# A decoder block on one core: other weight-ring depth and instruction order in the U stage, another one-hot layout, groups of 4 at the end of V, more gathers in U

## The chip, the cores and the metric

The kernel runs on one core of a Trainium2 chip. The metric is the device time in microseconds (us) of one execution. The core has one matrix engine (TensorE, "PE" in the profile, with its weight loads as "PEld"), a vector engine (VectorE, "DVE"), a scalar engine (ScalarE, "ACT"), GpSimd ("POOL") and SyncE ("SP"), which here only issues DMAs. Each engine works through its own list of instructions in order.

## The reference, cut to what matters

The block is attention and an mLSTM side by side, an output projection, and then PEER, a product-key mixture of 16,384 one-row experts, which takes some two thirds of the time:

```python
q  = (ht @ w_q).reshape(T, HEADS, 2, SUB)              # T = 528 token rows, 512 of which are output
s  = einsum('thpd,hpnd->thpn', q, sub_keys)            # scores of 2 x 128 sub-keys per head
...                                                    # top 16 of each side, then top 16 of the sums
idx, gate                                              # (T, 8 heads x 16), gate = softmax of the best
act = gelu(einsum('td,tkd->tk', hb, u[idx]))           # u, v: 16384 x 2048 f32
y   = einsum('tk,tkd->td', gate * act, v[idx])
out = rmsnorm(x + y)
```

## The kernel before, in words

Two ways of computing PEER stand side by side. 352 of the tokens go the dense way: all 16,384 experts are computed for them on TensorE, and a gate matrix G (expert x token, nearly all zero) picks the right ones. The other 128 + 32 tokens go the sparse way: for each of their picks POOL gathers one expert row per partition (L836, 128 rows of 8 KB, about 1.05 MB) and DVE multiplies it with the token and sums (L844, "dot"), or adds it with a weight to the result (L857, "axpy"). There are 320 such gather steps (NJ), first those of u, then those of v. A planner (`run`, `pace`, JU) spreads them: JU of them are to be done by the end of the U stage, the rest in V. At most 3 rows are in flight (buffers "ug").

The dense way has two stages.

*U* goes through 128 chunks of 128 experts. For each chunk `step` computes u·h for 352 tokens with 48 f32 matmuls (16 k-tiles, each as high·high, low·high and high·low part of the operands, L89 to L91), `u_chunk` applies GELU on ACT (L889) and stores the result to DRAM (Ad, L890). The weights come in two halves of 512 KB a chunk: `load_half` issues the DMA on SP (L72) into one of 3 raw buffers, `split_half` makes the high part on ACT (L79, `hid`) and the low part on DVE (L80, `lod`); 5 buffers each for high and low. Chunks 0 to 31 run beside the routing (top-k; `t2b` and `t3` sum the ids out of one-hots on POOL, L969, and DVE, L974). Chunks 32 to 121 ("U main") carry the building of G: a group of 4 tokens at a time, `ebuild` makes one-hot matrices `e` (is_equal, L1076 and L1077), the weighted `eg` on DVE (L1079) and `ea` on ACT (L1081), and `gbuild` multiplies them on TensorE (12 bf16 matmuls of 128 columns, L1092), copies the product on ACT to a staging tile `stg` (L1093, a single buffer of 2 MB) and every 8 groups stores it to DRAM (Gd, L1095). Chunks 122 to 127 (UTAIL) run beside the first preparations of V.

*V* goes through 256 halves of v. For each group of chunks (GROUPS) the operands act = GELU x G are loaded from Ad and Gd (`p_load`: gt, av), multiplied (`p_mul`: tm) and split (`p_split`: ah, al). All groups but the last run in transposed form (`tmm`: 24 matmuls of 352 columns a half, the weights being the v half); at the end of a group `yadd` adds the PSUM banks to yT on DVE (L1287). The last group runs in row form (`vmm`: token rows out, 18 matmuls of 512 columns a half), and `part` and `finish` turn its sums into the normalized output.

The order of most engines is set by a scheduler inside the program; POOL is in written order from U main on. With the change ACT is, too. The kernel's functions that the diff touches:

Of the kernel before, what the change touches and what calls it, by code (L numbers as in the profile page):

```python
# [8 lines left out]
F = mybir.dt.float32  # L9
# [5 lines left out]
OP = mybir.AluOpType  # L15
# [26 lines left out]
NQ = 128 // NB  # L42
SB = 128 // NQ
ND = S - 128 - NB
GROUPS = [8] + [16] * 7 + [8]
NJ = 2 * (128 + SB)
JU = 150
AR = 20
AR1 = 8

# [1 line left out]
def bcast(ap, n):  # L52
    return bass.AP(tensor=ap.tensor, offset=ap.offset, ap=[list(a) for a in ap.ap] + [[0, n]])
# [7 lines left out]
def body(tc, I, out):  # L61
    nc = tc.nc
    top = ExitStack()
    with top:
# [3 lines left out]
        dp = top.enter_context(tc.tile_pool(name="dp", bufs=1, space=DRAM))  # L68

        def load_half(src, name, rawp=None):  # L70
            raw = (rawp or wp).tile([128, 8, 128], F, name="raw" + name, tag="raw", bufs=3)
            nc.sync.dma_start(raw, src.rearrange("p (k c) -> p k c", k=8))  # L72
            return raw

        def split_half(src, name, raw=None, eng=nc.vector):
            raw = raw or load_half(src, name)
            hi = wp.tile([128, 8, 128], R, name="hi" + name, tag="whi")
            lo = wp.tile([128, 8, 128], R, name="lo" + name, tag="wlo")
            nc.scalar.copy(hi, raw)  # L79
            eng.tensor_tensor(lo, raw, hi.bitcast(F), op=OP.subtract)  # L80
            return hi, lo

        def split_tile(src, name):
            return [split_half(src[b], f"{name}_{b}") for b in range(2)]

        def mm3(ps, w, k, xh, xl, cs):
            hi, lo = w[k // 8]
# [578 lines left out]
def rest(tc, I, out, L):  # L666
# [204 lines left out]
    sp = [I["wq"][i] for i in range(16)] + [I["u"][c] for c in range(NK)]  # L871
    w[2] = split_tile(sp[2], "d2")

    def step(n, mid=None):
        if n + 1 < len(sp):
            w[n + 1] = split_tile(sp[n + 1], f"d{n + 1}")
        ps = pmu.tile([128, 512], F, name="pu", tag="pu")
        nn = S if n < 16 else ND
        for k in range(KD):
            mm3(ps[:, :nn], w[n], k, h2h, h2l, slice(0, nn))  # L880
            if k == 7 and mid:
                mid()
        w.pop(n)
        return ps

    def u_chunk(c, mid=None):
        ps = step(16 + c, mid)
        at = h2p.tile([128, ND], F, name="at", tag="at", bufs=3)
        nc.scalar.activation(at, ps[:, :ND], AF.Gelu)  # L889
        nc.scalar.dma_start(Ad[c // 4, :, c % 4, :], at)  # L890

    with tc.tile_pool(name="tk", bufs=1) as tk, \
            tc.tile_pool(name="pss", bufs=2, space=PSUM) as pss, \
# [33 lines left out]
        def head_tasks(h, b):  # L927
            st = {}
            cs = slice(16 * h, 16 * h + 16)

            def grid(dst, lo, hi):
                o = 0
                for i in range(5):
                    n = 16 // (i + 1)
                    nc.gpsimd.tensor_tensor(dst[:, o:o + n], lo[:, :n], bcast(hi[:, i], n), op=OP.add)
                    o += n
                nc.gpsimd.tensor_tensor(dst[:, o:o + 6].rearrange("p (a c) -> p a c", c=2), bcast_mid(lo[:, :2], 3),
                                        bcast(hi[:, 5:8], 2), op=OP.add)
                nc.gpsimd.tensor_tensor(dst[:, o + 6:o + 14], hi[:, 8:16], bcast(lo[:, 0], 8), op=OP.add)

            bv = (gsel if b == 3 else gs[:, b])[:, cs]

            def t1():
                sv = tk.tile([128, 2, 16], F, name="sv", tag="sv", bufs=3)
                si = tk.tile([128, 2, 16], U32, name="si", tag="si", bufs=3)
                st["sv"], st["si"] = sv, si
                return [(sv[:, p, :], si[:, p, :], hd[h, p][:, b, :]) for p in range(2)]

            def t1b():
                sv, si = st["sv"], st["si"]  # L950
# [12 lines left out]
            def t2b():
                bpb = tk.tile([128, 16], BF, name="bpb", tag="bpb", bufs=3)
                nc.vector.tensor_copy(bpb, st["bp"])
                eq = tk.tile([128, NCAND, 16], BF, name="eqb", tag="eqb", bufs=2)
                nc.vector.tensor_tensor(eq, iom, bcast_mid(bpb, NCAND), op=OP.is_equal)
                oh = tk.tile([128, NCAND, 16], F, name="oh", tag="oh", bufs=2)
                nc.gpsimd.tensor_tensor(oh, eq, bcast(st["cd"][:, 1, :], 16), op=OP.mult)  # L969
                st["oh"] = oh  # L970

            def t3():
                oh = st["oh"]
                nc.vector.tensor_reduce(ids[:, b, cs], oh.rearrange("p c k -> p k c"), axis=AX.X, op=OP.add)  # L974
# [88 lines left out]

    with tc.tile_pool(name="gk", bufs=1, reuse_waits="tile") as gk, \
            tc.tile_pool(name="psg", bufs=2, space=PSUM) as psg, \
            tc.manual_schedule(engines={mybir.EngineType.Pool}):
        stg = {}

        ge = {}

        def ebuild(q):
            t0 = 4 * q
            e = gk.tile([128, 2, 128, 4], BF, name="e", tag="e", bufs=2)
            eg = gk.tile([128, 2, 128, 4], BF, name="eg", tag="eg", bufs=2)
            ea = gk.tile([128, 4, 128], BF, name="ea", tag="ea", bufs=2)
            nc.vector.tensor_tensor(e[:, 0], iota4, bcast_mid(n1T[:, t0:t0 + 4], 128), op=OP.is_equal)  # L1076
            nc.vector.tensor_tensor(e[:, 1], iota4, bcast_mid(n2T[:, t0:t0 + 4], 128), op=OP.is_equal)  # L1077
            for i in range(2):
                nc.vector.tensor_tensor(eg[:, i], e[:, 1], bcast_mid(gp[:, 1 + i, t0:t0 + 4], 128), op=OP.mult)  # L1079
            for j in range(4):  # L1080
                nc.scalar.activation(ea[:, j, :], e[:, 1, :, j], AF.Copy, scale=g0[:, t0 + j:t0 + j + 1])  # L1081
            ge[q] = e[:, 0], [ea.rearrange("p j n -> p n j"), eg[:, 0], eg[:, 1]]

        def gbuild(q):
            tg, r = divmod(4 * q, TG)
            if r == 0:
                stg[tg] = gk.tile([128, NK, TG], F, name="stg", tag="stg")
            e1, eg = ge.pop(q)
            pg = psg.tile([128, 4, 128], F, name="pg", tag="pg")
            for j in range(4):  # L1090
                for i in range(3):
                    nc.tensor.matmul(pg[:, j, :], e1[:, :, j], eg[i][:, :, j], start=(i == 0), stop=(i == 2))  # L1092
            nc.scalar.copy(stg[tg][:, :, r:r + 4], pg.rearrange("p j n -> p n j"))  # L1093
            if r + 4 == TG:
                nc.sync.dma_start(Gd[tg, :, 0:NK, :], stg[tg])  # L1095
# [6 lines left out]
        ebuild(0)  # L1102

        def pace(c):
            run(n0 + int((c + 1 - c0) * (JU - n0) / (NK - c0)))

        for c in range(ci, NK - UTAIL):
            u_chunk(c)
            while ng < min(ND // 4, (c + 1 - ci) * (ND // 4) / (NK - 12 - ci)):
                gbuild(ng)  # L1110
                ng += 1
                if ng < ND // 4:
                    ebuild(ng)
            pace(c)
    sU.close()

    with ExitStack() as sV:
        vp = sV.enter_context(tc.tile_pool(name="vp", bufs=1, side="right", reuse_waits="tile"))
        pool_order = sV.enter_context(tc.manual_schedule(engines={mybir.EngineType.Pool}))
        g0s = [sum(GROUPS[:g]) for g in range(len(GROUPS) + 1)]  # L1120
        gts, ats, tms, A = {}, {}, {}, {}

# [70 lines left out]
        for c in range(NK - UTAIL, NK):  # L1193
# [270 lines left out]
```

## Time and profile before

| what | us |
|---|---|
| median of 3 runs (lowest, highest) | 3330.11 (3321.87, 3330.35) |
| profiled execution, time | 3331.74 |
| profiled execution, span of the trace | 3330.0 |
| PE busy, share of span | 3264.0, 98% |
| DVE busy | 2320.2, 70% |
| ACT busy | 1325.5, 40% |
| POOL busy | 943.9, 28% |
| DMA traffic | 815.47 MB, mean 245 GB/s |

In stages, by the trace: projections, attention, mLSTM and the query projection until about 1000 us; routing beside U chunks until 1412; U main until 2210; UTAIL until 2264; V in transposed form until 3239.9; the row form of the last group until 3317; then the last normalization and store. Mean granted TensorE clock is 0.992 of full. PE's busy time is a union of pipelined matmuls, so the distance from start to start, not the duration of one, tells what an instruction costs the engine.

### The profile page before, as it was taken

How to read it: one execution, taken by the hardware profiler on the slowest of the kernel's cores; microseconds unless marked ns; L12 is line 12 of the kernel's file. 1: busy time of each engine (PE TensorE's matmuls, PEld its weight loads, DVE VectorE, ACT ScalarE, POOL GpSimd, SP SyncE). 2: the span in 40 equal slices, each digit the busy share in tenths (PEclk: the TensorE clock that was granted, in tenths of full speed). 3: DMA queues.
4: the chain of work that ended last, by engine and by line, in shares of the span. 5: the costliest groups of instructions: out<-in, count | busy, mean ns of one | idle time of the engine just before them, and what ended most of it. 6: DMA issues, size and time to landing. Idle time of an engine off the chain costs nothing.

```text
span 3330.0 us, 51020 instructions
## 1 busy us (share of the span) xinstructions
PE 3264.0 (98%) x20126; PEld 3067.1 (92%) x20126; DVE 2320.2 (70%) x3504; ACT 1325.5 (40%) x2219; POOL 943.9 (28%) x942
## 2 busy tenths in 40 slices
PE   8999999999999999999999999997999999999998
PEld 7889898888887899999999999997999999999996
DVE  7444444444367788787877778767888888888973
ACT  5444444453252233444544544433333333333323
POOL 2011111110015566423332233322323323323312
PEclk8999999999999999999999999998999999999999
DMA  4222121123353266588888978999999999999972
GB/s 154 70 70 77 64 77 64 64 70 115 127 186 136 87 221 226 206 323 316 332 343 325 361 297 348 354 362 337 377 354 375 372 365 370 375 364 372 379 279 101
DMA packets 230162, 815.47 MB, mean 245 GB/s; under 512 B 21697, under 2 KB 85697, under 8 KB 186529
## 3 DMA queue, kind: packets, MB, share of 16 engines
q1 hardware_dynamic: 105488, 400.72, 33.3%
q0 software_dynamic: 46080, 335.56, 25.7%
q10 hardware_dynamic: 78352, 75.92, 6.8%
q8 instruction: 158, 2.59, 0.3%
q14 instruction: 84, 0.68, 0.1%
HBM read 757.33 MB, written 54.79 MB: 244 GB/s over the span
## 4 chain that ended last, share of the span: by engine, by line
PE 85%; DVE 8%; DMA 2%; issue 2%; ACT 1%; POOL 1%; ACTq 0%; SPq 0%; POOLq 0%; DVEq 0%
PE pu L89 10%; PE pu L90 10%; PE pu L91 10%; PE py L1275 8%; PE py L1277 8%; PE py L1276 8%; PE ps L89 5%; PE ps L91 5%; PE ps L90 5%; PE pg L1092 3%; PE po L742 2%; PE po L740 2%; PE po L741 2%; DVE y L857 1%; DVE lov L80 1%
## 5 line engine op out<-in xcount | busy, mean ns | idle before, releaser
L89 PE MATMUL pu<-hh,hid 128*128 128x352 f32 (+1 forms) x2272 | 759.8, 334 | 0.2 <-ACT at L889 0.2
L90 PE MATMUL pu<-hh,lod 128*128 128x352 f32 (+1 forms) x2272 | 751.3, 331 | 3.1 <-DVE lod L80 3.1
L91 PE MATMUL pu<-hl,hid 128*128 128x352 f32 (+1 forms) x2272 | 750.2, 330 | 0.0
L1275 PE MATMUL py<-ah,hiv 128*128 128x352 f32 x1920 | 627.0, 327 | 20.5 <-ACT hiv L79 9.5
L1276 PE MATMUL py<-ah,lov 128*128 128x352 f32 x1920 | 623.4, 325 | 8.8 <-DVE lov L80 8.8
L1277 PE MATMUL py<-al,hiv 128*128 128x352 f32 x1920 | 625.5, 326 | 0.0
L79 ACT CAST hiv<-rawv 128x1024 fp32r<-128x1024 f32 x256 | 269.2, 1053 | 572.4 <-PE py L1277 462.6
L80 DVE TENSOR_TENSOR lod<-rawd,hid 128x1024 fp32r<-128x1024 f32 x284 | 361.0, 1287 | 176.7 <-ACT hid L79 175.5
L90 PEld LDWEIGHTS pu<-hh,lod 128*128 128x128 f32 x2272 | 428.2, 188 | 12.8 <-DVE lod L80 3.4
L89 PEld LDWEIGHTS pu<-hh,hid 128*128 128x128 f32 x2272 | 429.9, 189 | 10.3 <-ACT at L889 0.8
L91 PEld LDWEIGHTS pu<-hl,hid 128*128 128x128 f32 x2272 | 428.1, 188 | 9.7
L79 ACT CAST hid<-rawd 128x1024 fp32r<-128x1024 f32 x284 | 297.8, 1050 | 347.2 <-DMA rawd<-in_u_dram 235.1
L89 PE MATMUL ps<-xh,hiz 128*128 128x256 f32 (+2 forms) x1280 | 410.9, 321 | 1.3 <-DVE qT L369 1.2
L836 POOL DMA_INDIRECT ug<-in_un_dram,idx x128 | 249.2, 1947 | 522.3 <-DVE ug L844 500.8
L91 PE MATMUL ps<-xl,hiz 128*128 128x256 f32 (+2 forms) x1280 | 392.8, 307 | 0.0
L90 PE MATMUL ps<-xh,loz 128*128 128x256 f32 (+2 forms) x1280 | 392.5, 307 | 0.0
L1275 PEld LDWEIGHTS py<-ah,hiv 128*128 128x128 f32 x1920 | 363.0, 189 | 24.2 <-issue 12.9
L1276 PEld LDWEIGHTS py<-ah,lov 128*128 128x128 f32 x1920 | 362.6, 189 | 11.8 <-DVE lov L80 11.8
L836 POOL DMA_INDIRECT ug<-in_vn_dram,idx x128 | 229.0, 1789 | 469.7 <-DVE y L857 444.3
L1277 PEld LDWEIGHTS py<-al,hiv 128*128 128x128 f32 x1920 | 361.9, 188 | 0.0
L80 DVE TENSOR_TENSOR lov<-rawv,hiv 128x1024 fp32r<-128x1024 f32 x256 | 313.4, 1237 | 33.7 <-ACT hiv L79 33.5
L857 DVE SCALAR_TENSOR_TENSOR y<-ug,act,y 128x2048 f32<-128x2048 f32 x127 | 298.3, 2349 | 14.8 <-DMA ug<-in_vn_dram,idx 14.8
(342 smaller groups left out, 5029.9 us busy)
## 6 DMA issues: line engine op xcount, KB each, us to landing
rawd<-in_u_dram SPq DMA_DIRECT2D x256, 512.0 KB
rawv<-in_v_dram SPq DMA_DIRECT2D x256, 512.0 KB
rawz<-in_wz_dram SPq DMA_DIRECT2D x98, 512.0 KB
Ad<-at ACTq DMA_DIRECT2D x128, 176.0 KB
Gd<-stg SPq DMA_DIRECT2D x11, 2048.0 KB
gt<-Gd ACTq DMA_DIRECT2D x32, 704.0 KB
av<-Ad ACTq DMA_DIRECT2D x64, 352.0 KB
rawwo<-in_wo_dram SPq DMA_DIRECT2D x40, 512.0 KB
```

The source lines that it names most:

```text
L79: nc.scalar.copy(hi, raw)
L80: eng.tensor_tensor(lo, raw, hi.bitcast(F), op=OP.subtract)
L89: nc.tensor.matmul(ps, a, xh[k][:, cs], start=(k == 0), stop=False)
L90: nc.tensor.matmul(ps, b, xh[k][:, cs], start=False, stop=False)
L91: nc.tensor.matmul(ps, a, xl[k][:, cs], start=False, stop=(k == KD - 1))
L740: nc.tensor.matmul(ps[tb], mh[n][:, sl], h, start=(n == 0), stop=False)
L836: nc.gpsimd.indirect_dma_start(out=t, out_offset=None, in_=I["un" if kind in "dD" else "vn"], in_offset=bass.IndirectOffsetOnAxis(ap=ix[:, ...
L857: nc.vector.scalar_tensor_tensor(acc[kind], t, o, acc[kind], op0=OP.mult, op1=OP.add)
L1092: nc.tensor.matmul(pg[:, j, :], e1[:, :, j], eg[i][:, :, j], start=(i == 0), stop=(i == 2))
L1275: nc.tensor.matmul(po, h, ah, start=(pr + j == 0), stop=False)
L1276: nc.tensor.matmul(po, l, ah, start=False, stop=False)
L1277: nc.tensor.matmul(po, h, al, start=False, stop=(2 * pr + j == n - 1))
```

## The change

Five edits, all in the second half of the kernel.

1. The last V group of 8 chunks becomes two groups of 4: four chunks change from row form to transposed form (halves in transposed form 240 to 248, in row form 16 to 8).
2. JU goes from 150 to 168, and the planner's pace is counted to the end of U main, not of UTAIL; UTAIL calls it no more.
3. In U main a second pool "ru" with 2 buffers makes the raw ring 5 deep instead of 3. The split of a chunk is written two chunks ahead, behind the GELU of the current one (`uload(c + 18)`), instead of one ahead, before its matmuls. ACT runs in written order in U main and V.
4. The one-hots are stored with 2 tokens interleaved instead of 4: `e` and `eg` are [2, 2, 128, 2] instead of [2, 128, 4], so a matmul of one token reads elements 2 apart instead of 4.
5. In the routing POOL adds the two halves of the product one-hot x id before DVE reduces it (25 candidates wide instead of 50).

```diff
-GROUPS = [8] + [16] * 7 + [8]
+GROUPS = [8] + [16] * 7 + [4, 4]
-JU = 150
+JU = 168
...
         def load_half(src, name, rawp=None):
-            raw = (rawp or wp).tile([128, 8, 128], F, name="raw" + name, tag="raw", bufs=3)
+            pool, n = rawp or (wp, 3)
+            raw = pool.tile([128, 8, 128], F, name="raw" + name, tag="raw", bufs=n)
...
+    ru = []
+
+    def uload(n):
+        if n < len(sp) and n not in w:
+            ps = [None, None]
+            if ru:
+                for b in range(2):
+                    if ru[1] % 5 in (1, 3):
+                        ps[b] = (ru[0], 2)
+                    ru[1] += 1
+            w[n] = split_tile(sp[n], f"d{n}", ps)
+
     def step(n, mid=None):
-        if n + 1 < len(sp):
-            w[n + 1] = split_tile(sp[n + 1], f"d{n + 1}")
+        uload(n + 1)
...
         nc.scalar.activation(at, ps[:, :ND], AF.Gelu)
         nc.scalar.dma_start(Ad[c // 4, :, c % 4, :], at)
+        if ru:
+            uload(c + 18)
...
                 nc.gpsimd.tensor_tensor(oh, eq, bcast(st["cd"][:, 1, :], 16), op=OP.mult)
-                st["oh"] = oh
+                nc.gpsimd.tensor_tensor(oh[:, 0:NCAND // 2], oh[:, 0:NCAND // 2], oh[:, NCAND // 2:], op=OP.add)
+                st["oh"] = oh[:, 0:NCAND // 2]
...
-            tc.manual_schedule(engines={mybir.EngineType.Pool}):
+            tc.manual_schedule(engines={mybir.EngineType.Pool, mybir.EngineType.Activation}), \
+            tc.tile_pool(name="ru", bufs=1, reuse_waits="tile") as rup:
         stg = {}
+        ru += [rup, 0]
...
+        def pairs(t):
+            a = [list(p) for p in t.ap]
+            return bass.AP(tensor=t.tensor, offset=t.offset, ap=[a[0], [2 * a[1][0], 2], [0, 128], [a[1][0], 2]])
...
-            e = gk.tile([128, 2, 128, 4], BF, name="e", tag="e", bufs=2)
-            eg = gk.tile([128, 2, 128, 4], BF, name="eg", tag="eg", bufs=2)
-            ea = gk.tile([128, 4, 128], BF, name="ea", tag="ea", bufs=2)
-            nc.vector.tensor_tensor(e[:, 0], iota4, bcast_mid(n1T[:, t0:t0 + 4], 128), op=OP.is_equal)
+            e = gk.tile([128, 2, 2, 128, 2], BF, name="e", tag="e", bufs=2)
+            eg = gk.tile([128, 2, 2, 128, 2], BF, name="eg", tag="eg", bufs=2)
+            ea = gk.tile([128, 2, 2, 128], BF, name="ea", tag="ea", bufs=2)
+            nc.vector.tensor_tensor(e[:, 0], iota2, pairs(n1T[:, t0:t0 + 4]), op=OP.is_equal)
...
-                nc.scalar.activation(ea[:, j, :], e[:, 1, :, j], AF.Copy, scale=g0[:, t0 + j:t0 + j + 1])
+                nc.scalar.activation(ea[:, j // 2, j % 2, :], e[:, 1, j // 2, :, j % 2], AF.Copy,
+                                     scale=g0[:, t0 + j:t0 + j + 1])
...
-                    nc.tensor.matmul(pg[:, j, :], e1[:, :, j], eg[i][:, :, j], start=(i == 0), stop=(i == 2))
+                    nc.tensor.matmul(pg[:, j, :], e1[:, j // 2, :, j % 2], eg[i][:, j // 2, :, j % 2],
+                                     start=(i == 0), stop=(i == 2))
...
         def pace(c):
-            run(n0 + int((c + 1 - c0) * (JU - n0) / (NK - c0)))
+            run(n0 + int((c + 1 - c0) * (JU - n0) / (NK - UTAIL - c0)))
...
+        ru.clear()
...
-        pool_order = sV.enter_context(tc.manual_schedule(engines={mybir.EngineType.Pool}))
+        pool_order = sV.enter_context(tc.manual_schedule(engines={mybir.EngineType.Pool, mybir.EngineType.Activation}))
...
-                                    None if i % 6 < 3 and i < nlast - 4 else vr[0])
+                                    None if i % 6 < 3 and i < nlast - 4 else (vr[0], 3))
...
             for _ in range(-(-len(pro) // (NK - c))):
                 f, q = pro.pop(0)
                 f(q)
-            pace(c)
```

The first place is ACT in the middle of U main, over one chunk and the start of the next. `hid_0` and `hid_1` are the high parts of a chunk's two halves. Before:

```order
L79 CAST hid_1_18759<-rawd_1_18757 128x1024
L889 ACTIVATE at<-pu 128x352
L79 CAST hid_0_18846<-rawd_0_18844 128x1024
L890 DMA Ad<-at 128x352
L1093 COPY stg<-pg 128x128x4
L1081 ACTIVATE ea<-e,g_9082 128x128 x4
```

After:

```order
L902 ACTIVATE at<-pu 128x352
L903 DMA Ad<-at 128x352
L80 CAST hid_0_17364<-rawd_0_17362 128x1024
L80 CAST hid_1_17370<-rawd_1_17368 128x1024
L1117 COPY stg<-pg 128x128x4
L1103 ACTIVATE ea<-e,g_9083 128x128 x4
```

The GELU now stands ahead of both casts, the casts are those of the chunk after the next, and the copy to the staging tile stands ahead of `ea` in both.

The second place is DVE in the same stretch. Before:

```order
L80 TENSOR_TENSOR lod_0_16206<-rawd_0_16203,hid_0_16205 128x1024
L80 TENSOR_TENSOR lod_1_16212<-rawd_1_16209,hid_1_16211 128x1024
L1076 TENSOR_TENSOR e<-iota_9077,n1T 128x512
L1077 TENSOR_TENSOR e<-iota_9077,n2T 128x512
L1079 TENSOR_TENSOR eg<-e,gp 128x512 x2
L844 SCALAR_TENSOR_TENSOR ug,act<-ug,h2n 128x2048
```

After:

```order
L81 TENSOR_TENSOR lod_0_16609<-rawd_0_16606,hid_0_16608 128x1024
L81 TENSOR_TENSOR lod_1_16615<-rawd_1_16612,hid_1_16614 128x1024
L1098 TENSOR_TENSOR e<-iota_9077,n1T 128x512
L1099 TENSOR_TENSOR e<-iota_9077,n2T 128x512
L1101 TENSOR_TENSOR eg<-e,gp 128x512 x2
L846 SCALAR_TENSOR_TENSOR ug,act<-ug,h2n 128x2048 x2
```

The sequence within a chunk is the same, with two dots behind it in more of the chunks; but the `lod` pair of a row belongs to a chunk one later than before.

The third place is ACT at the passage from U main to UTAIL, where the first operands of V are loaded. Before:

```order
L1128 DMA gt<-Gd 128x11x128
L79 CAST hid_1_21900<-rawd_1_21898 128x1024
L1131 DMA av<-Ad 128x704 x2
L1128 DMA gt<-Gd 128x11x128
L889 ACTIVATE at<-pu 128x352
L79 CAST hid_0_21964<-rawd_0_21962 128x1024
```

After:

```order
L902 ACTIVATE at<-pu 128x352
L903 DMA Ad<-at 128x352
L1153 DMA gt<-Gd 128x11x128
L1156 DMA av<-Ad 128x704 x2
L80 CAST hid_0_22371<-rawd_0_22369 128x1024
L80 CAST hid_1_22377<-rawd_1_22375 128x1024
```

Before, the first gt load stood four GELUs ahead of the first `ah`, in U main; after, the first gt load stands behind the GELU of chunk 122. DVE's first product of it stands like this. After:

```order
L859 SCALAR_TENSOR_TENSOR yB<-ug,wB,yB 128x2048 x2
L1160 TENSOR_TENSOR tm<-av,gt 128x352
L81 TENSOR_TENSOR lod_0_22372<-rawd_0_22369,hid_0_22371 128x1024
L81 TENSOR_TENSOR lod_1_22378<-rawd_1_22375,hid_1_22377 128x1024
```

So the low parts of chunk 124's weights are queued behind the product that needs this load.

## Rows read from the trace of the kernel before

**Rows 1.** The page's chain that ended last, shares of the span by engine.

```profile
PE 85%; DVE 8%; DMA 2%; issue 2%; ACT 1%; POOL 1%; ACTq 0%; SPq 0%; POOLq 0%; DVEq 0%
```

**Rows 2.** Stages: window, its us, busy of PE, PEld, DVE, ACT, POOL, clock, DMA share, GB/s.

```profile
1000.00:1412.00 412.00, 404.27 (x2259) 376.12 (x2258) 329.95 (x981) 134.67 (x216) 229.49 (x470) 1.00 0.50 175
1412.00:2210.00 798.00, 797.43 (x5376) 785.25 (x5376) 618.99 (x787) 380.58 (x717) 247.09 (x125) 1.00 0.87 334
2210.00:2264.00 54.00, 48.74 (x290) 47.63 (x288) 36.63 (x43) 18.68 (x27) 16.18 (x8) 0.97 0.91 345
2264.00:2380.00 116.00, 99.93 (x564) 96.65 (x565) 84.39 (x96) 42.10 (x67) 32.22 (x19) 0.93 0.94 351
2380.00:3190.00 810.00, 798.72 (x4914) 795.58 (x4914) 710.21 (x655) 259.45 (x303) 265.05 (x148) 1.00 0.97 368
3236.00:3318.00 82.00, 81.72 (x396) 63.92 (x395) 34.40 (x41) 26.54 (x45) 19.86 (x15) 1.00 0.33 114
```

**Rows 3.** PE's waits in U main (1412 to 2210): us in total, times, longest.

```profile
PE pg L1092 <- DVE eg L1079: 0.3, 1, 0.3
PE pg L1092 <- ACT ea L1081: 0.2, 1, 0.2
```

**Rows 4.** PE timeline in one gbuild: start, us, operation.

```profile
1806.35 0.25 PE L1092 MATMUL pg<-ea,e 128*128 128x128 bf16 x1
1806.43 0.40 PE L1092 MATMUL pg<-eg,e 128*128 128x128 bf16 x2
1806.65 0.24 PE L1092 MATMUL pg<-ea,e 128*128 128x128 bf16 x1
```

**Rows 5.** Instruction groups in U main: busy us, mean ns, idle before.

```profile
L844 DVE SCALAR_TENSOR_TENSOR ug<-ug,h2n 128x2048 f32<-128x2048 f32 x113 | 256.0, 2286 | 1.3 <-DMA ug<-in_un_dram,idx 1.3
L80 DVE TENSOR_TENSOR lod<-rawd,hid 128x1024 fp32r<-128x1024 f32 x181 | 218.1, 1222 | 109.9 <-ACT hid L79 109.1 <-issue 0.7
L1092 PEld LDWEIGHTS <-e 128*128 128x128 bf16 x1056 | 95.1, 117 | 12.7 <-issue 1.1
L1079 DVE TENSOR_TENSOR eg<-e,gp 128x512 bf16<-128x512 bf16 x176 | 67.0, 422 | 3.0
```

**Rows 6.** The same view, 0 to 1000 us: contiguous bf16 weights.

```profile
L424 PEld LDWEIGHTS <-identb 128*128 128x128 bf16 x64 | 6.1, 96 | 4.1 <-issue 0.6
```

**Rows 7.** ACT's waits in U main.

```profile
ACT hid L79 <- DMA rawd<-in_u_dram: 218.0, 105, 9.0
ACT stg L1093 <- DMA Gd<-stg: 32.0, 9, 6.2
```

**Rows 8.** One Gd store: SP timeline (issue), then ACT's (the copy that waits).

```profile
1818.64 0.33 SPq L1095 DMA_DIRECT2D Gd<-stg  x1
...
1831.99 0.59 ACT L1093 COPY stg<-pg 128x512 f32<-128x512 f32 x1 [3.80 <-DMA Gd<-stg]
```

**Rows 9.** DMA of U main, all queues.

```profile
DMA packets 61333, 266.74 MB, mean 334 GB/s; under 512 B 6567, under 2 KB 20775, under 8 KB 43863
```

**Rows 10.** PE's waits from UTAIL into V (2210 to 2380).

```profile
PE py L1276 <- DVE lov L80: 8.8, 9, 2.2
PE py L1275 <- ACT hiv L79: 7.2, 1, 7.2
```

**Rows 11.** Two windows of 10 us at the passage, columns as in rows 2.

```profile
2270.00:2280.00 10.00, 5.92 (x37) 5.63 (x35) 0.53 (x2) 1.36 (x5) 1.04 (x2) 1.00 1.05 404
2280.00:2290.00 10.00, 6.29 (x20) 5.92 (x21) 6.36 (x6) 5.47 (x6) 1.70 (x1) 0.51 0.49 182
```

**Rows 12.** PE's waits in V (2380 to 3240).

```profile
PE py L1275 <- DVE yT L1287: 8.9, 10, 1.0
```

**Rows 13.** PE timeline in the row form of the last group.

```profile
3309.59 0.39 PE L1304 MATMUL py<-hiv,ah 128*128 128x512 f32 x1
3309.82 0.40 PE L1305 MATMUL py<-lov,ah 128*128 128x512 f32 x1
```

**Rows 14.** The routing's product one-hot x id: duration min/median/max.

```profile
L969 POOL TENSOR_TENSOR oh<-eqb,cd x32: 1544/1553/2546, 998.6 to 1381.9; 128x800 f32<-128x800 bf16 x32
```

More of the change, by code (lines that the diff above doesn't have):

```diff
@@ L70, in load_half, with split_half @@
         def load_half(src, name, rawp=None):
-            raw = (rawp or wp).tile([128, 8, 128], F, name="raw" + name, tag="raw", bufs=3)
+            pool, n = rawp or (wp, 3)
+            raw = pool.tile([128, 8, 128], F, name="raw" + name, tag="raw", bufs=n)
             nc.sync.dma_start(raw, src.rearrange("p (k c) -> p k c", k=8))
             return raw
-        def split_half(src, name, raw=None, eng=nc.vector):
-            raw = raw or load_half(src, name)
+        def split_half(src, name, raw=None, eng=nc.vector, rawp=None):
+            raw = raw or load_half(src, name, rawp)
             hi = wp.tile([128, 8, 128], R, name="hi" + name, tag="whi")
@@ L81, in split_half, with split_tile @@
             return hi, lo
-        def split_tile(src, name):
-            return [split_half(src[b], f"{name}_{b}") for b in range(2)]
+        def split_tile(src, name, rawps=(None, None)):
+            return [split_half(src[b], f"{name}_{b}", rawp=rawps[b]) for b in range(2)]
         def mm3(ps, w, k, xh, xl, cs):
@@ L819, in rest @@
     nc.scalar.dma_start(iota, I["c_iota"])
-    iota4 = up.tile([128, 128, 4], BF, name="iota4")
-    nc.vector.tensor_copy(iota4, bcast(iota, 4))
+    iota2 = up.tile([128, 2, 128, 2], BF, name="iota2")
+    for i in range(2):
+        nc.vector.tensor_copy(iota2[:, i], bcast(iota, 2))
     n1T = up.tile([128, ND], BF, name="n1T")
@@ L1065, in rest @@
             tc.tile_pool(name="psg", bufs=2, space=PSUM) as psg, \
[L1066 removed]
+            tc.manual_schedule(engines={mybir.EngineType.Pool, mybir.EngineType.Activation}), \
+            tc.tile_pool(name="ru", bufs=1, reuse_waits="tile") as rup:
         stg = {}
+        ru += [rup, 0]
         ge = {}
+        def pairs(t):
+            a = [list(p) for p in t.ap]
+            return bass.AP(tensor=t.tensor, offset=t.offset, ap=[a[0], [2 * a[1][0], 2], [0, 128], [a[1][0], 2]])
         def ebuild(q):
             t0 = 4 * q
[L1073 to L1077 removed]
+            e = gk.tile([128, 2, 2, 128, 2], BF, name="e", tag="e", bufs=2)
+            eg = gk.tile([128, 2, 2, 128, 2], BF, name="eg", tag="eg", bufs=2)
+            ea = gk.tile([128, 2, 2, 128], BF, name="ea", tag="ea", bufs=2)
+            nc.vector.tensor_tensor(e[:, 0], iota2, pairs(n1T[:, t0:t0 + 4]), op=OP.is_equal)
+            nc.vector.tensor_tensor(e[:, 1], iota2, pairs(n2T[:, t0:t0 + 4]), op=OP.is_equal)
             for i in range(2):
[L1079 removed]
+                nc.vector.tensor_tensor(eg[:, i], e[:, 1], pairs(gp[:, 1 + i, t0:t0 + 4]), op=OP.mult)
             for j in range(4):
[L1081 to L1082 removed]
+                nc.scalar.activation(ea[:, j // 2, j % 2, :], e[:, 1, j // 2, :, j % 2], AF.Copy,
+                                     scale=g0[:, t0 + j:t0 + j + 1])
+            ge[q] = e[:, 0], [ea.rearrange("p a b n -> p a n b"), eg[:, 0], eg[:, 1]]
         def gbuild(q):
```

## Prediction, made before the changed kernel had run

> **What bounds the kernel now.** First the chain that ended last [rows 1]: 85% of it is PE, so a saving counts only where it shortens PE's list or a time in which PE waits. Second the stages [rows 2], which show where PE waits at all. In U main (1412 to 2210) PE is busy 797.43 of 798 us: 90 chunks, 8.87 us each. At the passage (2210 to 2380) it is busy 148.7 of 170. In V's long stretch it is busy 798.72 of 810, with the DMA engines at a share of 0.97 and 368 GB/s; in U main they stand at 0.87 and 334. In the row form at the end PE is busy throughout. Third PE's waits: in U main 0.5 us in all [rows 3], so that stage gets shorter only by fewer or quicker PE instructions; at the passage the first V halves come late [rows 10]; in V some 9 us go to yT at group ends [rows 12].
>
> The sums are made against the profiled execution, 3331.74 us; the median of the runs shown is 3330.11, so 1.6 us come off at the end.
>
> **Layout of the one-hots (edit 4).** One token in `gbuild` takes 0.30 us of PE: from the `ea` matmul to the first `eg` one 0.08, then 0.22 for two `eg` [rows 4]. `ea` lies contiguous per token, `eg` is read 4 elements (8 bytes) apart; all multiply the same one-hot. So a strided operand costs 0.11 against 0.08. The change halves the distance to 2 elements. If 4 bytes stream like contiguous, two matmuls save 0.03 each: 0.06 a token, 0.24 a group, and 88 groups (1056 weight loads at 12 a group [rows 5]) give 21 us. At the low end nothing is saved. At the high end the weights, which come at the same stride, load faster too: 117 ns here [rows 5] against 96 contiguous [rows 6], 0.02 x 1056 = 22 us more, if loads show in the distance at all. The `ea` matmul with its strided weights goes at 0.08 already, so I take none of that. I take -18, near the 21 with a little left for 4 bytes not being contiguous; ends 0 and -41.
>
> [...]
>
> On DVE `e` and `eg` keep 4 instructions of 512 elements, 422 ns as for `eg` [rows 5], but the innermost run goes from 4 to 2 elements. Nothing shows such a run. Bounds: 0, or f32's pace, 1222 ns for 1024 [rows 5], 0.61 for 512, +0.19 x 4 = 0.76 us a group. I take 0, the row of the same operation and type. ACT's `ea` writes contiguously in both: 0.
>
> **U main's load (edits 2 and 3).** The pace now puts 153 gathers instead of 126 into these 90 chunks. DVE: 27 x 2.29 [rows 5] = 62, so 681 of some 788 us. That is 86%, 95% with the 0.76 above: enough in both, with little slack. DMA: 266.74 MB [rows 9] plus 27 x 1.05 less two gt loads (1.4) is 294 MB, and in 788 us 373 GB/s. Scaled by the share, 334/0.87 = 384 is what the mix could give; V reached 368. So U main goes close to its DMA limit. The 5-deep ring keeps more halves in flight: before, ACT waited 218 us for raw halves [rows 7] though PE never did.
>
> The order has its price. In a chunk ACT now does GELU, two casts, copy, `ea`; DVE two `lod`, four one-hots, two dots. The `lod` pair can start only after this chunk's GELU, and `e` follows it, so `e` and `ea` are done some 6 us into a period of 8.7 (GELU and casts 1.7, `lod` 2.4, four one-hots 1.7 less overlap), where before they had up to a chunk more. And the copy to `stg` waits for the Gd store before it: 13.35 us from issue to copy here [rows 8], nine waits in all, the longest 6.2 [rows 7]; `ea`, and the next GELU, stand behind it. I cost the order at +8 us: eleven stores with under 1 us each that reach PE. Ends 0 (the ring covers all) and +48 (rival C).
>
> So U main: 798 - 18 + 8 = 788, -10.
>
> **UTAIL and the passage.** UTAIL loses 54 - 288 x 0.1625 = 7.2 us and V's first 116 us lose 116 - 564 x 0.1625 = 24.4, with 0.1625 = 798.72/4914 as the distance of f32 matmuls [rows 2]. What is late are V's first halves: low parts 8.8 us, one high part 7.2 [rows 10]. [...] The change takes out what competes there: UTAIL had 9 gathers (9.4 MB and 9 dots), and now has none. Before V's first loads the queues then hold only raw halves. I leave 8 of the 24.4: -16.5; ends 0 and -24.
>
> In UTAIL the gt load, which stood four GELUs ahead of its product before (some 35 us at 8.87 a chunk), is now issued directly ahead of it, and a `lod` pair is queued on DVE behind that product. The load waits for the whole G (2 MB stores, 13 us [rows 8]) and takes some us itself; chunk 123's low parts are ready by then, so PE has one chunk of cover, 7.8 us. I take one stall of 5 us instead of the 7.2 lost now, and no dots there: -3; ends -7 and +8.
>
> **V.** 152 gathers instead of 170, over 248 halves instead of 240: 0.61 a half instead of 0.71. DVE and DMA get lighter (710 of 810 and 0.97 now), but PE waits only 11.3 us there, 8.9 of it at ten steps at group ends [rows 12], and there is one group end more. 0; ends -6 and +4.
>
> **The last group (edit 1).** A chunk in row form is 36 matmuls at 0.23 [rows 13], 8.4 us; transposed it is 48 at 0.1625, 7.8. Four chunks: -2.4. The seeds from yT stay. The end chain works the same tiles in 40 us instead of 80, with DVE 34, ACT 27 and POOL 20 us busy in the row form now [rows 2]: it fits, and may cost up to +3.
>
> **Ids (edit 5).** POOL adds 32 instructions of half the width of 1.55 us [rows 14], 0.8 each, DVE saves as much. Both stand beside PE, which is busy 404 of 412 us there [rows 2]: 0; ends -2 and +2.
>
> **Sum:** -10 - 3 - 16.5 + 0 - 2.4 + 0 = -32: 3331.7 - 32 = 3299.8, less 1.6 for the median about 3298. I say 3300.
>
> **Rivals.** A: the distance 0.11 isn't the stride but the weights or PE's own pace, and `gbuild` stays at 0.30. For it: weight loads of 117 ns are longer than either distance, so something else than streaming may set them. Against: contiguous `ea` between two loads of the same kind goes at 0.08. Without the 18: 3316. [...]
>
> B: U main turns DMA-bound. At V's 368 GB/s [rows 2] 294 MB take 799 us instead of 788, and the passage starts with full queues, 4 more: 3298 + 15 = 3313. For it: the share of 0.97 in V. Against: in V PE, not DMA, sets the pace, so 368 is no ceiling.
>
> C, the slower side: the written order on ACT turns the wait for Gd stores into PE waits. Copy, `ea` and the next GELU stand behind the store. If a store is issued at time 0, the `gbuild` that needs the blocked `ea` starts some 2 x 8.7 - 1.2 = 16.2 us later; less the copy's 0.59 [rows 8], four `ea` (I take 0.4 each, as `eg` takes on DVE) and some 1.2 of hand-overs, a store may last about 12.8 before PE feels it. What is over comes to PE once per store, ten times (eleven stores). At 17 us, 4.2 x 10 = 42 and the sum is 3298 + 42 = 3340; from 16 us on it eats the whole gain (32). For it: the store shown lasts 13.35 already [rows 8], and U main's DMA share goes up from 0.87 to some 0.97. Against: the deeper ring takes raw halves off the critical moments, and in the present order 32 us of such waits on ACT [rows 7] leave PE 0.5.
>
> D: the passage isn't cured: gt, now late, and the first halves in written order on ACT keep the 19.5 us (16.5 and 3): 3317. For it: `gt` and the casts now stand in one line on ACT. Against: there are no gathers left to compete.
>
> **Chances and range.** Forecast 0.55 (3288 to 3312), A 0.17, B 0.10, C 0.10, D 0.08. A measurement can tell 0.3%, 10 us, from no change, so faster is below 3320 and slower above 3340. Nearly all of the forecast, most of A, B and D lie below 3320: 0.74. The same: C's lower half and where A, B and D add up, 0.15. Slower: C's upper half, and a sum of two, 0.11. The range 3280 to 3328: its low end takes half of the weights' 22 us and the order at nothing (8), its high end A or D with half of the other.
>
> **What would show it.** Layout: in `gbuild` `eg` to `eg` at 0.08, 0.24 us a token instead of 0.30, or unchanged (A). U main: some 788 us, DMA share 0.95 or more; waits `pg <- ea` or `pg <- eg` of some us right after Gd stores. If these sum to over 30, C holds; if PE waits for `hid` or `lod`, B. Passage: no 7 us wait for `hiv`, no clock of 0.5. One wait of PE for `lod` in UTAIL behind `tm`. Wrong altogether I'd be if PE's waits in U main exceed what the layout gives.

## The result, and the profile after

The changed kernel takes 3350.47 us (median of 6 runs, 3343.96 to 3355.41); the kernel before took 3330.12 in the same comparison. The ratio is 1.0065, interval [1.0049, 1.0081]: slower by some 20 us, where 3300 was forecast, and outside the range.

Where the 20 us lie, from the first `gbuild` matmul, the last matmul of chunk 121, the first and the last matmul of V in both traces:

| stretch | before | after | difference |
|---|---|---|---|
| start to first `gbuild` | 1419.5 | 1420.2 | +0.7 |
| U main, to the end of chunk 121 | 790.4 | 810.9 | +20.5 |
| UTAIL, to V's first matmul | 54.1 | 59.0 | +4.9 |
| V, to the last matmul | 1053.3 | 1046.9 | -6.4 |
| last normalization and store | 12.6 | 13.7 | +1.1 |

The stages of the changed kernel, columns as in [rows 2]:

```profile
1420.00:2231.00 811.00, 770.93 (x5330) 757.60 (x5329) 667.74 (x825) 372.99 (x706) 245.58 (x149) 0.97 0.92 355
2231.00:2290.00 59.00, 50.18 (x291) 49.35 (x289) 28.70 (x31) 18.23 (x26) 4.70 (x5) 0.91 0.79 281
2290.00:2406.00 116.00, 104.83 (x614) 103.66 (x615) 88.40 (x84) 44.55 (x70) 27.39 (x16) 0.94 0.92 336
2406.00:3200.00 794.00, 781.12 (x4786) 777.95 (x4785) 646.56 (x617) 245.54 (x294) 210.96 (x123) 1.00 0.91 340
```

U main, where PE had been busy all the time, now has 40 us in which it isn't, at a mean clock of 0.97. The DMA share rose only to 0.92. PE's waits there, against the 0.5 us of [rows 3]:

```profile
PE pg L1115 <- ACT ea L1103: 20.6, 6, 4.9
PE pg L1115 <- DVE eg L1101: 19.3, 4, 4.9
```

These are few and long: nine stalls of 3.6 to 4.9 us, and one wait of 0.2. Yet `gbuild` itself, the same view as [rows 4], got much quicker:

```profile
1795.88 0.23 PE L1115 MATMUL pg<-ea,e 128*128 128x128 bf16 x1
1795.94 0.28 PE L1115 MATMUL pg<-eg,e 128*128 128x128 bf16 x2
1796.06 0.22 PE L1115 MATMUL pg<-ea,e 128*128 128x128 bf16 x1
```

A token takes 0.18 us instead of 0.30, the `ea` matmul 0.06 instead of 0.08, a group 0.66 instead of 1.11: 0.45 x 88 = 40 us less. The weight loads got shorter too (min/median/max in ns, before and after):

```profile
L1092 PEld LDWEIGHTS <-e x1056: 111/115/136, 1419.5 to 2163.8; 128*128 128x128 bf16 x176
L1115 PEld LDWEIGHTS <-e x1056: 96/97/152, 1420.2 to 2185.0; 128*128 128x128 bf16 x176
```

So the stalls and what hangs on them cost 20.5 + 40 = 60 us.

They are of two kinds. Five follow a store of G. SP's timeline at one (the store's issue), then ACT's (an idle time and its end in brackets), then PE's:

```profile
1481.84 1.50 SPq L1119 DMA_DIRECT2D Gd<-stg  x1
```

```profile
1487.51 2.00 ACT L80 CAST hid<-rawd 128x1024 fp32r<-128x1024 f32 x2 [0.40 <-ACT at L902]
1498.98 0.59 ACT L1117 COPY stg<-pg 128x512 f32<-128x512 f32 x1 [9.47 <-DMA Gd<-stg]
1499.47 1.28 ACT L1103 ACTIVATE ea<-e,g 128x128 bf16<-128x128 bf16 x4
```

```profile
1499.92 0.26 PE L1115 MATMUL pg<-ea,e 128*128 128x128 bf16 x1 [4.88 <-ACT ea L1103]
```

The copy waits 9.5 us for the store, 17.1 us from the store's issue to the copy; `ea` stands behind it, and PE behind `ea`. That is rival C.

Four are of a kind that the prediction doesn't have. The 88 groups go into 84 chunks, so four chunks have two groups, and the second one's one-hots are only written behind the first. DVE's timeline at one, then PE's:

```profile
1806.44 2.36 DVE L81 TENSOR_TENSOR lod<-rawd,hid 128x1024 fp32r<-128x1024 f32 x2
1808.72 0.42 DVE L1098 TENSOR_TENSOR e<-iota,n1T 128x512 bf16<-128x512 bf16 x1
1809.06 0.41 DVE L1099 TENSOR_TENSOR e<-iota,n2T 128x512 bf16<-128x512 bf16 x1
1809.51 0.76 DVE L1101 TENSOR_TENSOR eg<-e,gp 128x512 bf16<-128x512 bf16 x2
```

```profile
1804.89 0.28 PE L1115 MATMUL pg<-eg,e 128*128 128x128 bf16 x2
1809.96 0.27 PE L1115 MATMUL pg<-ea,e 128*128 128x128 bf16 x1 [4.79 <-DVE eg L1101]
```

The first group ends at 1805; `e` of the second stands on DVE behind low parts that need this chunk's GELU and casts. Behind each of the nine stalls the granted clock is 0.50 for another 2.9 to 6.0 us. Around this one:

```profile
1804.00:1809.00 5.00, 1.17 (x15) 0.86 (x14) 4.87 (x7) 2.94 (x4) 3.80 (x2) 0.87 0.93 335
1809.00:1811.00 2.00, 1.04 (x9) 0.99 (x10) 1.93 (x7) 1.28 (x4) 0.00 (x0) 0.50 1.00 393
1811.00:1815.00 4.00, 4.00 (x20) 4.00 (x18) 4.00 (x5) 1.76 (x5) 0.79 (x1) 0.55 1.01 418
1815.00:1819.00 4.00, 4.00 (x27) 4.00 (x25) 1.15 (x2) 0.00 (x0) 2.89 (x2) 1.00 0.60 190
```

At this one, of 4.8 us, the clock stays at 0.50 until about 1814.6: in the 4 us from 1811 on, 20 matmuls start, and 27 in the next four. In PE's busy time the nine come to 21 us (770.93 here, 750.00 in e9, below), 2.3 each, so by my estimate a stall of 4.8 us costs some 7 here.

In UTAIL and at the start of V (2240 to 2420), PE's longest waits, and what DVE did at the one for `lod`:

```profile
PE py L1299 <- ACT yT L1309: 10.8, 2, 6.1
PE pu L91 <- DVE lod L81: 8.2, 1, 8.2
```

```profile
2253.82 0.52 DVE L1160 TENSOR_TENSOR tm<-av,gt 128x352 f32<-128x352 f32 x1 [9.92 <-DMA av<-Ad]
2254.27 2.35 DVE L81 TENSOR_TENSOR lod<-rawd,hid 128x1024 fp32r<-128x1024 f32 x2
```

The product waits 9.9 us for its load and the low parts stand behind it, as foreseen; the price was 8.2, not 5. At the first group ends in V the copies to yT are late; ACT there:

```profile
2318.77 4.43 ACTq L1156 DMA_DIRECT2D av<-Ad  x1
2323.31 1.04 ACT L80 CAST hiv<-rawv 128x1024 fp32r<-128x1024 f32 x1 [4.54 <-issue]
...
2327.42 1.51 ACT L1309 COPY yT<-py 128x352 f32<-128x352 f32 x4
```

Issuing this load held ACT for 4.4 us; in written order the cast, and the copy that frees PE's banks, stand behind it. Later in V (2420 to 3340) PE waits as long again at group ends, now for DVE's sums into yT:

```profile
PE py L1299 <- DVE yT L1311: 11.0, 8, 3.2
```

### The profile page after: what moved, and what is told of

It is laid out like the page before. It is cut to its first block, busy times and chain, and to the rows that moved or that the text cites. A ratio compares the mean times of both kernels' runs of the same rounds, so it can differ in the third digit from the quotient of the medians.

```text
span 3350.7 us, 51178 instructions
## 1 busy us (share of the span) xinstructions
PE 3242.1 (97%) x20170; PEld 3054.6 (91%) x20174; DVE 2322.8 (69%) x3521; ACT 1313.9 (39%) x2219; POOL 904.2 (27%) x974
## 4 chain that ended last, share of the span: by engine, by line
PE 64%; issue 17%; DVE 7%; POOL 7%; DMA 3%; ACT 2%; ACTq 0%; SPq 0%; POOLq 0%; DVEq 0%
PE py L1299 7%; PE py L1301 7%; PE py L1300 7%; PE ps L90 5%; PE ps L92 5%; PE ps L91 5%; PE pu L90 5%; PE pu L91 5%; PE pu L92 5%; POOL ug L838 4%; PE po L743 2%; PE po L741 2%; PE po L742 2%; DVE y L859 1%; DVE lov L81 1%
## 5 line engine op out<-in xcount | busy, mean ns | idle before, releaser
L1299 PE MATMUL py<-ah,hiv 128*128 128x352 f32 x1984 | 648.4, 327 | 23.1 <-DVE yT L1311 11.0
L1301 PE MATMUL py<-al,hiv 128*128 128x352 f32 x1984 | 646.7, 326 | 0.0
L1300 PE MATMUL py<-ah,lov 128*128 128x352 f32 x1984 | 644.0, 325 | 1.5 <-DVE lov L81 1.4
L1299 PEld LDWEIGHTS py<-ah,hiv 128*128 128x128 f32 x1984 | 375.6, 189 | 26.6 <-issue 11.6
L838 POOL DMA_INDIRECT ug<-in_vn_dram,idx x128 | 219.7, 1717 | 593.7 <-DVE y L859 565.8
L1300 PEld LDWEIGHTS py<-ah,lov 128*128 128x128 f32 x1984 | 375.2, 189 | 2.6 <-DVE lov L81 2.6
L1301 PEld LDWEIGHTS py<-al,hiv 128*128 128x128 f32 x1984 | 374.4, 189 | 0.0
L838 POOL DMA_INDIRECT ug<-in_un_dram,idx x128 | 206.0, 1609 | 488.6 <-DVE ug L846 469.0
L80 ACT CAST hid<-rawd 128x1024 fp32r<-128x1024 f32 x284 | 288.0, 1047 | 123.6 <-PE pu L92 56.0
L846 DVE SCALAR_TENSOR_TENSOR ug<-ug,h2n 128x2048 f32<-128x2048 f32 x128 | 298.9, 2356 | 19.6 <-DMA ug<-in_un_dram,idx 19.6
```

Source lines behind the costliest of these rows:

```text
L838: nc.gpsimd.indirect_dma_start(out=t, out_offset=None, in_=I["un" if kind in "dD" else "vn"], in_offset=bass.IndirectOffsetOnAxis(ap=ix[:, ...
L846: nc.vector.scalar_tensor_tensor(t, t, 1.0, acc[kind], op0=OP.mult, op1=OP.mult, accum_out=o)
L1299: nc.tensor.matmul(po, h, ah, start=(pr + j == 0), stop=False)
L1300: nc.tensor.matmul(po, l, ah, start=False, stop=False)
L1301: nc.tensor.matmul(po, h, al, start=False, stop=(2 * pr + j == n - 1))
```

## The experiments

The runs are called e1 to e15. Each result is a median in us, with its ratio to the kernel before in the same comparison and a 95% interval of the ratio.

**The edits by themselves, on the kernel before.** e1, edit 4 alone (the layout's lines of the diff above):

> The kernel before with the one-hot layout alone (edit 4). If the layout is worth what the trace of the changed kernel shows (a group of 12 matmuls in 0.64 us instead of 1.06, 88 groups, 37 us) and the old order hides the rest as it did, 3293. If a shorter chunk uncovers another engine or the DMA in U main in the old order too, so that the stalls have nothing to do with the new order, 3312 to 3330.

It takes 3305.96, ratio 0.9933 [0.9916, 0.9949]. U main takes 768.6 instead of 790.4: 22 of the 40 us arrive. PE waits 14 us there, 11 of it for the GELU's release of its bank. So the layout gains in the old order too, and a part of it is lost again to waits that weren't there before.

e10, edit 1 alone:

```diff
-GROUPS = [8] + [16] * 7 + [8]
+GROUPS = [8] + [16] * 7 + [4, 4]
```

> The kernel before with the two last V groups of 4 alone (edit 1). By the prediction's term 3330 - 2.4 = 3328. If the groups also remove the waits for yT at group ends (12 us before, none in e4), 3316.

It takes 3312.15, ratio 0.9957 [0.9944, 0.997]: V is 1033.9 instead of 1053.3. The waits of [rows 12] shrink to

```profile
PE py L1275 <- DVE yT L1287: 1.9, 3, 0.9
```

so the term -2.4 was far too small. Of the 19 us, some 6 lie in V's first 116, where 599 matmuls start instead of 564, and 9 in the 811 behind them, where PE is idle 2.1 us instead of 11.3. The groups also change the step at which each of V's gathers falls due (`nlast` sets the pace); that this is what clears them is not shown.

e11, edits 1 and 4:

> The kernel before with the layout and the groups of 4 (edits 4 and 1), everything else as before. If they add: e1's 3306 less what e10 gains, 3294 to 3304.

It takes 3291.45, ratio 0.9897 [0.9881, 0.9914]: they add. e15, edit 5 alone (the line on `oh`):

> The kernel before with the ids' half sum on GpSimd alone (edit 5). By the prediction 0: 3327 to 3333. If POOL becomes what the routing waits for (32 x 0.8 us more on POOL), up to 3350; if DVE is what it waits for, 3315 to 3325.

It takes 3330.75, ratio 1.0014 [1.0004, 1.0024], which is inside the 0.3% over which the kernel before ranges in that comparison (3323.32 to 3332.69).

**U main's order, on the changed kernel.** e2, no double groups:

```diff
-            while ng < min(ND // 4, (c + 1 - ci) * (ND // 4) / (NK - 12 - ci)):
+            while ng < min(ND // 4, (c + 1 - ci) * (ND // 4) / (NK - 8 - ci)):
```

> The changed kernel with the 88 groups of G spread over 88 chunks instead of 84, so that no chunk has two. Theory 1 (the second group of a double chunk needs one-hots that DVE can only make after this chunk's GELU, casts and low parts): four stalls of 5.0 us and the low clock behind each (some 2.5 us) go, 3350 - 30 = 3320. Rival (the stalls come from stores and DMA traffic, wherever the groups stand): 3345 to 3352.

It takes 3328.6, ratio 0.9994 [0.9983, 1.0005], 22 less than the changed kernel. The second kind of stall is gone; the first is not, and costs 7 us more than it did:

```profile
PE pg L1115 <- ACT ea L1103: 27.8, 6, 5.4
PE pg L1115 <- DVE eg L1101: 1.3, 4, 0.4
```

e3, the copy behind `ea`:

```diff
-            nc.scalar.copy(stg[tg][:, :, r:r + 4], ...)    # in gbuild
+            return pg                                      # the copy and the store in gcopy
...
-                gbuild(ng)
+                pg = gbuild(ng)
                 ng += 1
                 if ng < ND // 4:
                     ebuild(ng)
+                gcopy(ng - 1, pg)
```

> The changed kernel with the copy into the staging tile written behind the next group's ea on ACT, so that a copy that waits for a store no longer holds up ea. Theory 2 (rival C of the prediction: store, then copy, then ea): five stalls of 3.9 to 5.2 us and the low clock behind them go, 3350 - 33 = 3317, and waits for the copy move to the GELU. Rival (the one-hots come late for another reason, or the late GELU and casts cost as much): 3340 to 3352.

It takes 3342.87, ratio 1.005 [1.0033, 1.0067]: 8 less than the changed kernel instead of 33. The rival was right; the releaser only changed its name:

```profile
PE pg L1115 <- DVE eg L1101: 40.2, 11, 6.6
```

The late copy now holds up the GELU, the casts behind it, and so the low parts behind which `e` stands. Both kinds of stall point to that place of `e`. e5, a first try to put it elsewhere (one-hots and `ea`, then casts, then the copy):

```diff
-        if ru:
-            uload(c + 18)                  # in u_chunk, ahead of the groups
...
                 if ng < ND // 4:
                     ebuild(ng)
+            uload(c + 18)
+            for q, pg in pgs:
+                gcopy(q, pg)
```

> The changed kernel with another order at the end of a U main chunk: the one-hots and ea of the next group first, then the casts and low parts of the chunk after the next, last the copy into the staging tile. Theory 4 (the ten stalls of U main have one root: e stands on DVE behind low parts that can only be made after this chunk's GELU and casts, so a chunk has less than 3 us in hand against double groups and late stores): nearly all of the 42 us of waits and the low clock behind them go, U main and UTAIL 870 to 815, total 3298. Rival (the casts or the late copy take the place of ea as the thing that comes late): 3325 to 3345.

It takes 3364.41, ratio 1.011 [1.0081, 1.0139]: worse than the changed kernel, and than both expectations. ACT, then DVE, in one chunk of it:

```profile
1710.10 1.28 ACT L1101 ACTIVATE ea<-e,g 128x128 bf16<-128x128 bf16 x4 [5.74 <-DVE e L1097]
1711.29 1.98 ACT L80 CAST hid<-rawd 128x1024 fp32r<-128x1024 f32 x2
```

```profile
1707.10 2.29 DVE L846 SCALAR_TENSOR_TENSOR ug<-ug,h2n 128x2048 f32<-128x2048 f32 x1
...
1709.65 0.42 DVE L1097 TENSOR_TENSOR e<-iota,n2T 128x512 bf16<-128x512 bf16 x1
1710.10 0.76 DVE L1099 TENSOR_TENSOR eg<-e,gp 128x512 bf16<-128x512 bf16 x2
1712.35 2.36 DVE L81 TENSOR_TENSOR lod<-rawd,hid 128x1024 fp32r<-128x1024 f32 x2 [1.49 <-ACT hid L80]
```

A ring has closed: two dots, `e` (DVE), `ea`, casts (ACT), low parts, dots (DVE). With two dots it takes 9.7 us a chunk, more than PE's 8.4, and PE waits for low parts in chunk after chunk; the second groups of the four chunks still wait beside that, some 22 us in all:

```profile
PE pu L91 <- DVE lod L81: 24.8, 37, 1.5
PE pg L1113 <- DVE eg L1099: 22.8, 5, 8.5
```

e7, with V's two edits (e4 and e6, below) on top:

> The last two edits together with ACT in the scheduler's order from UTAIL on (the run before with that edit alone gave 3320.7). If the three losses are separate places of the program, they add: 3350.5 - 29.8 - 52 - 11 = 3258 at best, and 3270 if the shorter U main hits the DMA limit (294 MB in 750 us are 392 GB/s; the most that windows of some us show is 417 to 427). If they are one loss seen twice, 3295.

It takes 3335.67, ratio 1.0021 [1.0011, 1.0032]: 29 less than e5, as e4's edit gives by itself, so U main and V add. But U main's ring stays (825.7 us), and the 3258 is missed by that.

e9 starts from this: the ring opens when the casts stand ahead of `ea` on ACT, while `e` stays ahead of the low parts on DVE. With e7's edits in V and one group a chunk:

```diff
                 if ng < ND // 4:
-                    ebuild(ng)
+                    bd = ebuild(ng)        # e, eg on DVE
+                    uload(c + 18)          # casts on ACT, low parts on DVE
+                    eabuild(ng, *bd)       # ea on ACT
             uload(c + 18)                  # does nothing where it is done
             for q, pg in pgs:
                 gcopy(q, pg)
```

> Built on e7: on DVE the one-hots of the next group stand first, then the low parts, as there; but on ACT the casts stand ahead of ea, so that no chain DVE (e) - ACT (ea, casts) - DVE (low parts) closes within a chunk, as e7 showed with chunks of 9.7 us; and one group a chunk. If the stalls of U main come from that order alone, U main and UTAIL are 90 x 8.4 + 47 = 803 us instead of 870, and with the free order in V 3350.5 - 29.8 - 55 = 3265. If the late store now holds up the casts instead (copy, then GELU, then casts), five to ten stalls of some us stay: 3290 to 3310.

It takes 3262.04, ratio 0.9811 [0.9789, 0.9833]: 67 us less than the kernel before, 88 less than the changed one. U main's stage, one of ACT's waits, and the DMA from 1412 to 2173:

```profile
1423.00:2173.00 750.00, 750.00 (x5331) 738.50 (x5330) 668.06 (x825) 367.57 (x706) 227.96 (x150) 1.00 0.98 384
```

```profile
ACT stg L1123 <- DMA Gd<-stg: 50.4, 10, 7.6
```

```profile
DMA packets 62150, 291.12 MB, mean 383 GB/s; under 512 B 6922, under 2 KB 18428, under 8 KB 41660
```

PE never waits in U main. The copies still wait 50 us for the stores, and it no longer reaches anyone; the same gathers pass, at 383 GB/s. The losses of the changed kernel were neither the stores' nor the DMA's own, but the order behind them.

e14, that order in U main alone, four chunks with two groups, V as changed:

> The changed kernel with e9's order in U main alone (four chunks still have two groups, V and its loads as changed). If the order is the whole of U main's loss, its stalls go except for the second groups of four chunks, which wait for casts and ea behind this chunk's GELU (some 2.5 us each with the low clock behind): U main 811 to 768, total 3307. If one group a chunk was what did it in e9, U main stays near 790 and the total near 3330.

It takes 3300.76, ratio 0.9922 [0.9905, 0.9939]; U main takes 771.4. So the order alone gives 39.5 of the 60 us back; with one group a chunk besides (e9), the rest. Five waits of PE are left, of 0.5 to 5.5 us, the four longest at the double groups:

```profile
PE pg L1117 <- DVE eg L1099: 8.2, 2, 5.5
PE pg L1117 <- ACT ea L1106: 5.2, 2, 2.7
```

**The ring of raw halves.** e13, e9 with 3 halves:

```diff
-                    if ru[1] % 5 in (1, 3):
-                        ps[b] = (ru[0], 2)
```

> The run e9 with the raw ring of 3 halves again instead of 5, all else the same. If the deeper ring carries the 168 gathers (in e12, with 3 halves and the old order, U main took 823 us), U main goes from 750 to 790 or more and the total from 3262 to 3300 or more, with ACT waiting for raw halves. If only the order does it, 3262 to 3270.

It takes 3333.55, ratio 1.001 [1.0, 1.002]: 71 us more than e9. U main takes 818.9, and ACT waits again:

```profile
ACT hid L80 <- DMA rawd<-in_u_dram: 276.5, 96, 6.6
```

e12, the changed kernel with the whole of edit 3 undone:

> The changed kernel with edit 3 undone (raw ring of 3, splits one chunk ahead, ACT in the scheduler's order throughout); layout, groups, 168 gathers and the ids as changed. Theory 4 (it is the order that loses, and the other edits gain or do nothing): 3290 to 3300, no wait of PE for pg over 1.5 us. If the 27 gathers more in U main are what makes the one-hots or the halves late, 3315 to 3330 with waits of PE for hid, lod or pg in U main.

It takes 3318.82, ratio 0.9978 [0.9967, 0.9989]. The rival held: U main takes 816.5, and ACT waits 349 us for raw halves; 126 gathers with the same order and ring took 764.1 (e11). So edit 3 has two sides: its 5 halves are what carries the 27 gathers more (by e13, in e9's order; the old order with 5 halves was not run), and its order throws that away.

**UTAIL and V, on the changed kernel.** e4, ACT by the scheduler from UTAIL on:

```diff
-        pool_order = sV.enter_context(tc.manual_schedule(engines={mybir.EngineType.Pool, mybir.EngineType.Activation}))
+        pool_order = sV.enter_context(tc.manual_schedule(engines={mybir.EngineType.Pool}))
```

> The changed kernel with ACT ordered by the scheduler again from UTAIL on (U main as changed). Theory 3 (written order on ACT puts the first gt load and the copies of yT behind other work): the wait of 8.7 us for lod in UTAIL and the waits of 6.4 and 5.0 us for yT at the first groups get small, with the low clock behind them 3350 - 20 = 3330. Rival (those are the DMA's: the loads would come late in any order): 3345 to 3352.

It takes 3320.66, ratio 0.9976 [0.9966, 0.9986], 30 less than the changed kernel. V takes 1018.9 instead of 1046.9:

```profile
2291.00:2407.00 116.00, 110.53 (x670) 108.10 (x671) 91.52 (x86) 46.85 (x70) 31.72 (x18) 1.00 0.92 339
2407.00:3200.00 793.00, 793.00 (x4896) 793.00 (x4895) 662.27 (x629) 258.89 (x300) 217.40 (x128) 1.00 0.93 349
```

The passage is cured (110.5 busy of 116, at a clock of 1.00) and PE waits for nothing after it. UTAIL's wait for low parts stayed (9.5 us), against the expectation. e6, for that one:

```diff
-            for _ in range(-(-len(pro) // (NK - c))):
+            for _ in range(4 if c == NK - UTAIL else -(-len(pro) // (NK - c))):
```

> The changed kernel with V's first loads (gt, av) in chunk 122 and the first product tm only in chunk 123, behind that chunk's low parts on DVE. Theory 3a (PE's wait of 8.7 us for lod in UTAIL is a low part queued behind a product that waits for its load): the wait goes with the low clock behind it, 3350 - 11 = 3339. Rival (the casts or raw halves would have been as late): 3347 to 3352.

It takes 3351.66, ratio 1.0064 [1.0039, 1.0089]: no gain on the changed kernel. The 8.2 us wait for `lod` becomes one of 4.6 for `hid` a chunk later and smaller ones. On ACT the casts of the next chunk stand behind `ah`, which waits for the same load; only the engine that hands on its lateness has changed. e8, e4's edit with 150 gathers instead of 168:

> The changed kernel with ACT in the scheduler's order from UTAIL on, and 150 gathers by the end of U main instead of 168. Tells why V's waits for yT at group ends vanished in that run (12 us in the kernel before, none there). If it is the smaller number of gathers a half in V, they come back, V is 12 us longer and U main's waits don't change: 3332. If it is the new buffers and groups, V stays and U main gains a little from its lighter load: 3315.

It takes 3314.1, ratio 0.9964 [0.9952, 0.9977]. That is the total of the second reading, but not by its way: U main gains only 4 us on e4 (809.9) and keeps its ten waits, V loses 5 (1024.1) though its group ends stay nearly clear (1.9 us of waits), and UTAIL loses its wait (48.4 instead of 59.6 in e4). So the group ends are not a matter of gathers, while the wait in UTAIL went with 18 gathers fewer ahead of it.

## Why the prediction was wrong

- **Layout, -18: right in sign, too small; -40.** The prediction set aside the weights' stride because the `ea` matmul went at 0.08 already. After, all three matmuls of a token go at 0.06, and the weight load takes 97 ns instead of 115, so the upper bound of -41 was the answer. A token took 0.30 us with its strided elements 8 bytes apart and takes 0.18 with 4. Rival A is out. DVE's 2-element runs cost nothing (421 ns for `eg`, 422 before).
- **Order in U main, "I cost the order at +8 us: eleven stores with under 1 us each that reach PE": the step that failed; +60.** Of the 60, five stores give 20.5, four double groups 19.2 (4.8 each, gone in e2), and the clock of 0.50 behind the nine stalls 21. Rival C named the stores' part of the mechanism and an end of +48, but got a chance of 0.10; its working adds 42 to a sum that holds the 8 already, so it comes to +50. Three things were missed: the double groups; that each stall takes some 2 us more behind it, at a clock of 0.50; and that a slack of 2.7 us (6 of 8.7 by the prediction; 1.9 in the trace, from the last `ea` at 1802.4 to `gbuild` at 1804.3) leaves nothing for either. Rival C's limit of 12.8 us was good: stores of 15.5 to 17.1 us from issue to copy make stalls, those of 12.4 and less don't. The prediction took one store of 13.35 for all; the nine of the kernel before on which a copy waits last 10.4 to 15.9 us, and four are over the limit.
- **DMA limit, rival B: no.** The DMA share is 0.92 in the changed kernel, and e9 moves the load at 383 GB/s with PE busy throughout. 368 was no ceiling, as the prediction argued.
- **UTAIL, -3: +4.9.** The stall foreseen came, 8.2 instead of 5, with its low clock (0.50 from 2256 to 2260).
- **Passage -16.5, V 0, last group -2.4, together -19: -6.4.** Here errors of both signs partly cancel: the groups are worth 19 us in V (e10), what else the change does in V 15 more (1018.9 in e4), and written order on ACT costs 28 (1046.9 against 1018.9 in e4; 1019.2 in e12, where it is undone throughout). Of the 15, some 10 are there with V's gathers as before and none in UTAIL (1024.1 in e8); that the gathers give them is likely, but e8 and e10 differ in other edits too, so it is not shown. Rival D put that order's price at the passage alone, 19.5.
- **Ids, 0: as said** (e15).

The terms as measured: U main -40 + 60, UTAIL +5, V -19 - 15 + 28, the ends +2, which is 21 of the 20.7 in the traces.

## What to carry to other kernels

Where an order is fixed by hand, go round each chain that passes between two engines within one iteration and add it up: what stands behind an instruction that can wait is as late as it, whichever engine it is on (here a copy's wait of 9.5 us on ACT came to PE as 4.9). Work that needs nothing of this iteration belongs ahead of work that does, and a wait that can be long belongs last. A deeper ring shows what it is worth only when nothing else is in line behind it (here 5 halves gave 71 us in e9's order, by e13, while the whole of edit 3 cost the changed kernel some 30, by e12); try buffers and order apart.

## What the runs showed of the hardware

- bf16 matmuls of 128 columns start 0.06 us apart where weights and `eg` are read 4 bytes apart, against 0.11 at 8 bytes, and 0.08 where only the weights were.
- Over 761 us the DMA engines moved 383 GB/s at a share of 0.98, with slices of 19 us up to 424.
- At each of nine stalls of 3.6 to 4.9 us in the changed kernel's U main the granted clock fell to 0.50, and it stayed there for 2.9 to 6.0 us after PE's next matmul began; PE is busy 770.93 us for 5330 matmuls there, in e9 750.00 for 5331, so the nine cost 21 us beside the 40 of waiting.
- Issuing one load of av held ACT's list for 4.8 us in UTAIL (at 2240) and 4.4 at the first group end in V (at 2319); over all 64 such loads the median is 0.6 and the longest 5.1. Why was not tried.
